# Hybrid streaming encoder step on one core: raw out-projection weights for two blocks, earlier operand loads, and five smaller moves

## The chip, the cores and the metric

The kernel runs on one core of a Trainium2 chip. The metric is the device time of one launch in microseconds, the median of the runs of a kernel. The kernel before has a median of 2514.28 us over three runs (2513.0 to 2514.96).

## The reference, cut to what matters

One layer for 2048 prompt frames and 8 streams of 16 new frames, 2176 tokens in all, in float32, with 1024 channels:

```
z = rmsnorm(x) @ w_in                       # 1280 columns: q 512, k 128, v 128, u 512
a = attention(q, k, v)                      # 8 heads of 64, own chunk of 64 frames + 128 before, sinks
b = pooled means of u (2/4/8/16 frames) - u, a linear map per group, a scale
x = x + concat(rmsnorm(a), rmsnorm(b)) @ w_out
x = x + square(relu(rmsnorm(x) @ w_up)) @ w_down        # 4096 hidden
x = x + sigmoid(rmsnorm(x) @ w_gate) * (p @ w_ple)
y = rmsnorm(x)
```

## The kernel before, in words

**Number format.** Each float32 product is made of three products of rounded halves: a matrix is split into a high part, rounded by ScalarE (a copy into the narrower type), and a low part, the rest, by a subtraction on VectorE or GpSimd. `split` does that for tokens and weights. `mm3` issues the three products of each 128x128 piece of weights. A unit is 128x512 numbers of weights (256 KB raw); its halves together are 512 KB.

**Phase A** (the first 750 us) works on six token blocks (256 and five of 384 tokens). Its steps stand in the string SEQ_A, a letter and a block each: P loads and squares x, I projects (10 output tiles), M takes buffers for the mixer output, A is attention (three tiles of 128 tokens for most blocks, 16 in all), K is pooling, B and R are norms of the mixer outputs, O is the out-projection (8 output tiles d, each of a pool half ps_ob and an attention half ps_oa) that adds x and writes the sum x1 to DRAM (x1d), F is the norm of x1, written to rsd. C0 to C3 (`comb_first`) build columns of the operands of the first up projection: they read x1d and rsd, scale, form sums and differences, split these seven ways and write them to DRAM (cd0). Each C takes the four row buffers xr for its rows and, from C0 to C3, two of the six raw weight buffers wr for the norms.

**Weights in phase A.** `load_w` splits raw weights for blocks 0 and 1. At block 1 it also writes both halves to DRAM (ws...), and blocks 2 to 5 read the halves back without splitting. Raw weights go through six wr buffers into five pairs of wh and wl; halves read back go straight into wh and wl.

**Phase B** works on three pairs of token halves (s = 0, 1, 2; 352 or 368 tokens a half). `up` makes seven products of sums of weights with the seven operands B11, T2, B21, T1, T3, B22, T4 instead of eight, `down` accumulates, `tail` applies the gate (ps_gt) with the embedding product (ps_ple), `finish` the final norm. The loads of the operands of s = 0 (14 tiles of 736 KB) start inside `out_proj(5)`: into buffers of phase B that come free when attention's buffers are released, and two of them into the twelve token buffers q4 of the pool `quads`, which also hold xn and mx.

**PSUM.** ps_ple and ps_gt take three buffers in turn (two mm, one pv) through `ps_dn`; the up products take two sc and two tr in turn.

**Order.** The framework puts each engine's instructions in order at compile time from a timeline of its own (schedule_with_timeline_sim=True), with the order of the program as priority, so the order in a trace is near that of the code, not equal to it. `issue_after` keeps an engine's instructions behind a given one of the same engine. Each engine runs its instructions in that order, and SyncE (SP) issues nearly all DMAs in that order.

Of the kernel before, what the change touches and what calls it, by code (L numbers as in the profile page):

```python
# [7 lines left out]
F32 = mybir.dt.float32  # L8
# [8 lines left out]
P = 128  # L17
# [6 lines left out]
NTOK = SEQ + NSAMP  # L24
BLOCKS = [256, 384, 384, 384, 384, 384]
STARTS = [sum(BLOCKS[:i]) for i in range(len(BLOCKS))]
SEQ_A = "I0 P1 M0 A0 K0 B0 S0 I1 P2 M1 K1 I2 B1 R0 A1 O0 P3 F0 R1 M2 K2 I3 B2 A2 O1 R2 M3 P4 F1 K3 O2 B3 A3 F2 P5 R3 I4 C0 M4 O3 A4 C1 F3 K4 I5 B4 C2 R4 M5 K5 C3 B5 A5 O4"
NXR = 4
TAGS = ("ms ms ms ms ms").split()
LOENG = [lambda nc: nc.vector]  # L30
# [44 lines left out]
def hymba_step(ctx: ExitStack, tc: tile.TileContext, ins, outs):  # L75
# [33 lines left out]
    def ps_tile(tag, nm):  # L109
        return pst.tile([P, 512], F32, tag=tag, name=nm, bufs=PS_BUFS[tag])  # L110

    cnt = [0]
    last_load = [None]

    dn_ring = [0]

    def ps_dn(nm):
        dn_ring[0] += 1
        return ps_tile(("mm", "mm", "pv")[dn_ring[0] % 3], nm)
# [23 lines left out]
    saved = {}  # L143

    def load_w(src, ktiles, key, b):
        if key in saved:
            units = []
            for dh, dl in saved[key]:
                hi = wp.tile([P, 4, P], F32R, tag="wh", name="whi", bufs=NWH)
                lo = wp.tile([P, 4, P], F32R, tag="wl", name="wlo", bufs=NWL)  # L150
                nc.sync.dma_start(out=hi.bitcast(F32), in_=dh)
                nc.sync.dma_start(out=lo.bitcast(F32), in_=dl)
                units.append((hi, lo))
            return WU(units)
        units = [load_u(src[:, k : k + 4, :]) for k in range(0, ktiles, 4)]
        if b == 1:
            saved[key] = []
            for i, (hi, lo) in enumerate(units):
                dh, dl = (dram.tile([P, 4, P], F32, name=f"ws{key}{i}{c}") for c in "hl")
                nc.sync.dma_start(out=dh, in_=hi.bitcast(F32))  # L160
                nc.sync.dma_start(out=dl, in_=lo.bitcast(F32))
                saved[key].append((dh, dl))
        return WU(units)

    def mm3(ps, whl, xs, first=True, last=True):
        n = len(xs)
        for i, (wk, (xh, xl)) in enumerate(xs):
            nc.tensor.matmul(ps, lhsT=whl.hi(wk), rhs=xh, start=first and i == 0, stop=False)  # L168
            nc.tensor.matmul(ps, lhsT=whl.lo(wk), rhs=xh, start=False, stop=False)  # L169
            nc.tensor.matmul(ps, lhsT=whl.hi(wk), rhs=xl, start=False, stop=last and i == n - 1)  # L170

    def ks(xt, N, kk):
        return [(k, (at8(xt[0], k)[:, :N], at8(xt[1], k)[:, :N])) for k in kk]
# [183 lines left out]
    def comb_first(k):  # L357
        wr = lambda dt: lambda nm, n: wp.tile([P, 512], dt, tag="wr", name=nm, bufs=NWR)[:, :n]
        comb(0, k, wr(F32R), wr(F32))

    def out_fin(b):
        rs = state[b]["sq1"].rstd(D, ps_tile("ms", "ps_ms"))
        nc.sync.dma_start(out=rsd[b], in_=rs)

    with tc.tile_pool(name="pa", bufs=2) as pa:
# [122 lines left out]
        def attn_tile(b, i):  # L488
            st_b = state[b]
            gt = TILE0[b] + i  # L490
            q0 = i * P
            qh, ql = st_b["q"]
            kh, kl = st_b["k"]
            first = gt == 0
            J = (1,) if first else (0, 1)
            c0 = 128 if first else 0
            nk = 256 - c0
            st = pa.tile([P, 4, 8], F32, tag="st", name="st")
            rmax, negm, den, esk = (st[:, j, :] for j in range(4))
            pt = []  # L500
            for kv in range(2):
                r = slice(kv * 64, kv * 64 + 64)
                pm = pa.tile([P, NQT, 256], F32, tag="pm", name="pm")
                pt.append(pm)
                for pr in range(2):
                    ps = ps_tile("sc", "ps_sc").rearrange("p (j k) -> p j k", j=2)
                    for j in range(2):
                        t = pr * 2 + j
                        o = ps[:, j, :nk]
                        kk = slice(q0 + c0, q0 + 256)  # L510
                        qq = slice(q0, q0 + 128)
                        nc.tensor.matmul(o, lhsT=qh[r, t, qq], rhs=kh[r, kk], start=True, stop=False)
                        nc.tensor.matmul(o, lhsT=ql[r, t, qq], rhs=kh[r, kk], start=False, stop=False)
                        nc.tensor.matmul(o, lhsT=qh[r, t, qq], rhs=kl[r, kk], start=False, stop=True)
                    for j in range(2):
                        t = pr * 2 + j
                        h = kv * 4 + t
                        nc.vector.tensor_tensor_reduce(
                            out=pm[:, t, :nk], in0=ps[:, j, :nk], in1=mask[:, c0:256], scale=1.0, scalar=NEG,
                            op0=ALU.add, op1=ALU.max, accum_out=rmax[:, h : h + 1],  # L520
                        )
                h4 = slice(kv * 4, kv * 4 + 4)
                nc.vector.scalar_tensor_tensor(
                    out=negm[:, h4], in0=rmax[:, h4], scalar=-0.125, in1=nsink[:, h4], op0=ALU.mult, op1=ALU.min
                )
                nc.vector.tensor_tensor(
                    out=esk[:, h4], in0=negm[:, h4], in1=nsink[:, h4], op=ALU.subtract
                )
                nc.scalar.activation(out=esk[:, h4], in_=esk[:, h4], func=AF.Exp)
                for t in range(4):  # L530
                    h = kv * 4 + t
                    nc.scalar.activation(
                        out=pm[:, t, :nk], in_=pm[:, t, :nk], func=AF.Exp, scale=0.125, bias=negm[:, h : h + 1],
                        accum_out=den[:, h : h + 1],
                    )
                nc.vector.tensor_tensor(out=den[:, h4], in0=den[:, h4], in1=esk[:, h4], op=ALU.add)
                nc.vector.reciprocal(out=den[:, h4], in_=den[:, h4])
                for t in range(4):
                    h = kv * 4 + t
                    nc.scalar.activation(  # L540
                        out=pm[:, t, :nk], in_=pm[:, t, :nk], func=AF.Copy, scale=den[:, h : h + 1]
                    )
            po = ps_tile("pv", "ps_pv")
            nmm = 2 * len(J) * 3
            n = 0
            for kv in range(2):
                for j in J:
                    tp = ps_tile("tr", "ps_tr").rearrange("p (t q) -> p t q", t=NQT)
                    for t in range(4):
                        nc.tensor.transpose(tp[:, t, :], pt[kv][:, t, j * 128 - c0 : j * 128 - c0 + 128], ident)  # L550
                    ph = pa.tile([P, NQT, P], F32R, tag="ph", name="ph")
                    pl = pa.tile([P, NQT, P], F32R, tag="pl", name="pl")
                    split(tp, ph, pl, nc.vector)
                    vi = (gt - 1 + j) % NVP
                    vh = vph[vi][:, kv * 64 : kv * 64 + 128]
                    vl = vpl[vi][:, kv * 64 : kv * 64 + 128]
                    for aa, bb in ((vh, ph), (vl, ph), (vh, pl)):
                        nc.tensor.matmul(po, lhsT=aa, rhs=bb, start=n == 0, stop=n == nmm - 1)
                        n += 1
            put_a(b, po.rearrange("p (t q) -> p t q", t=NQT), q0)  # L560
# [166 lines left out]
        def pool(b):  # L727
# [9 lines left out]

        acts = {
            "P": prologue, "I": in_proj, "M": mixers, "A": attn, "K": pool, "S": lambda b: attn_sample(b, NPR[b]),
            "R": out_ra, "B": out_rb, "O": out_proj, "F": out_fin, "C": comb_first,  # L740
        }
        prologue0()
        consts()
# [3 lines left out]
    with tc.tile_pool(name="pb", bufs=2) as pb:  # L747
# [18 lines left out]

        ops, acc, hq, x2, sqs, rs2 = {}, {}, {}, {}, {}, {}
        up_ring = [0]
        free[Q1] -= 4

        def comb_load(s, names):
            n = HN[2 * s]
            for o in names:
                ops.setdefault(s, {})[o] = (take(o + "h"), take(o + "l"))
                for t, d in zip(ops[s][o], comb_dram[s][o]):
                    nc.sync.dma_start(out=t[:, :, :n].bitcast(F32), in_=d)
# [135 lines left out]
        def tail(s, h, fill=()):  # L914
# [6 lines left out]
            for d in range(KT):  # L921
                if d % 2 == 0:
                    wpl = WU([load_u(w_ple[d // 2], eng=nc.gpsimd)])
                whl = WU([load_u(w_gate[d][:, 4 * i : 4 * i + 4, :], eng=nc.gpsimd) for i in range(2)])
                pe = ps_dn("ps_ple")[:, :n]
                mm3(pe, wpl, [(2 * (d % 2) + k, pt[k]) for k in range(2)])
                ps = ps_dn("ps_gt")[:, :n]
                mm3(ps, whl, xs)
# [38 lines left out]
        def loads(s, names):  # L967
            return [lambda o=o: comb_load(s, [o]) for o in names]

        out_proj(5, loads(0, OPS[:4]))  # L970
        comb_load(0, OPS[4:])
        free[Q1] += 4
        acc_load(0)
        for s in range(3):
# [7 lines left out]
            if s:  # L982
                finish(2 * s - 1)
                acc_load(s)
            else:
                out_fin(4)
                out_fin(5)
            up(s, 2)
            for c in range(NPAIR // 2 - 1):
                down(s, c)  # L990
# [140 lines left out]
```

## Time and profile before

| what | value |
|---|---|
| median of three runs | 2514.28 us |
| the profiled execution, its own time | 2511.46 us |
| its span, first to last instruction | 2509.7 us |
| mean granted TensorE clock | 0.975 |
| matrix products (PE instructions) | 13748 |
| DMA bytes | 370.63 MB |

A page of the profile gives busy times by engine and what ended an engine's idle time. PE is TensorE, DVE VectorE, ACT ScalarE, POOL GpSimd, SPq the DMA queue of SyncE. A wait is put down to the instruction or DMA that came last. The clock is a share of 2.4 GHz.

### The profile page before, as it was taken

The page shows a single profiled execution, that of the slowest core. Times are in us where ns is not written, and L with a number is a line of the kernel's source. Part 1 is how long each engine was busy: PE and PEld are TensorE (multiplying, and loading weights), DVE is VectorE, ACT ScalarE, POOL GpSimd, SP SyncE. Part 2 cuts the span into 40 slices and gives each one's busy share as a digit, 9 for nine tenths or more (in the row PEclk, how much of TensorE's full clock was granted, in tenths as well). Part 3 has the DMA queues.
Part 4 walks back from the last instruction along what each step waited for, and adds up shares of the span by engine and source line. Part 5 has one row for each costly group of instructions (what it writes and reads, how often), then busy time and mean ns, then how long its engine had stood idle before and what let it go on. Part 6 is the DMA issues. An engine that isn't in the chain of part 4 may idle for free.

```text
span 2509.7 us, 38994 instructions
## 1 busy us (share of the span) xinstructions
PE 2354.3 (94%) x13748; PEld 2266.9 (90%) x13748; DVE 1651.0 (66%) x2960; ACT 1025.7 (41%) x2151; POOL 1109.3 (44%) x938
## 2 busy tenths in 40 slices
PE   7789999999769999999999999999999999999986
PEld 7779888887669999999988999999988999999985
DVE  6656676655628777756767677776567766666555
ACT  6437665445413333322644233332354333333353
POOL 5614356342634444433565344443375433333363
PEclk9889999999889999999999999999999999999998
DMA  7945477776892333422644333432445422222232
GB/s 190 305 139 164 159 248 237 236 243 229 282 333 93 122 122 122 134 68 68 224 135 154 94 122 124 127 127 75 133 161 168 134 76 69 76 77 80 71 101 85
DMA packets 242164, 370.63 MB, mean 148 GB/s; under 512 B 43953, under 2 KB 119473, under 8 KB 241969
## 3 DMA queue, kind: packets, MB, share of 16 engines
q1 hardware_dynamic: 241424, 367.42, 45.7%
q8 instruction: 109, 1.79, 0.3%
q14 instruction: 87, 0.70, 0.1%
q10 hardware_dynamic: 544, 0.72, 0.1%
HBM read 298.49 MB, written 69.55 MB: 147 GB/s over the span
## 4 chain that ended last, share of the span: by engine, by line
PE 63%; DVE 14%; DMA 9%; issue 5%; POOL 4%; ACT 4%; SPq 1%; DVEq 0%; POOLq 0%; ACTq 0%
PE ps_dn L168 8%; PE ps_dn L169 8%; PE ps_dn L170 8%; PE ps_up L168 7%; PE ps_up L170 7%; PE ps_up L169 7%; POOL wlo L180 3%; PE ps_in L168 2%; PE ps_in L169 2%; PE ps_in L170 2%; DMA x<-in_xT 2%; DVE wlo L180 2%; DVE x2l L245 1%; DVE acc L856 1%; DMA xc<-x1d 1%
## 5 line engine op out<-in xcount | busy, mean ns | idle before, releaser
L168 PE MATMUL ps_dn<-hh,whi 128*128 128x368 f32 (+1 forms) x1536 | 505.8, 329 | 11.9 <-DVE acc L856 11.3
L169 PE MATMUL ps_dn<-hh,wlo 128*128 128x368 f32 (+1 forms) x1536 | 503.3, 328 | 0.0
L170 PE MATMUL ps_dn<-hl,whi 128*128 128x368 f32 (+1 forms) x1536 | 501.1, 327 | 0.0
L180 POOL TENSOR_TENSOR wlo<-wraw,whi 128x512 fp32r<-128x512 f32 x251 | 343.8, 1373 | 304.0 <-ACT whi L179 245.8
L856 DVE TENSOR_TENSOR acc<-ps_dn,acc 128x368 f32<-128x368 f32 (+1 forms) x384 | 201.8, 531 | 273.2 <-PE ps_dn L170 273.1
L179 ACT CAST whi<-wraw 128x512 fp32r<-128x512 f32 x384 | 236.6, 619 | 330.9 <-PE ps_dn L170 91.0
L168 PEld LDWEIGHTS ps_dn<-hh,whi 128*128 128x128 f32 x1536 | 288.4, 188 | 20.9 <-DVE acc L856 19.5
L180 POOL TENSOR_TENSOR wlo<-A,whi 128x512 fp32r<-128x512 f32 x96 | 127.4, 1327 | 373.2 <-ACT whi L179 268.2
L169 PEld LDWEIGHTS ps_dn<-hh,wlo 128*128 128x128 f32 x1536 | 288.5, 188 | 0.3
L170 PEld LDWEIGHTS ps_dn<-hl,whi 128*128 128x128 f32 x1536 | 288.5, 188 | 0.3
L179 ACT CAST whi<-A 128x512 fp32r<-128x512 f32 x192 | 119.1, 621 | 273.2 <-PE ps_dn L170 185.4
L168 PE MATMUL ps_in<-xnh,whi 128*128 128x384 f32 (+1 forms) x480 | 164.3, 342 | 19.4 <-ACT whi L179 7.7
L198 POOL TENSOR_TENSOR sqa<-sqa,sqt 128x384 f32<-128x384 f32 (+3 forms) x119 | 129.2, 1087 | 92.1 <-ACT sqt L197 84.0
L169 PE MATMUL ps_in<-xnh,wlo 128*128 128x384 f32 (+1 forms) x480 | 163.5, 341 | 1.5 <-DMA wlo<-wsi40l 0.9
L179 ACT CAST whi<-S 128x512 fp32r<-128x512 f32 x144 | 89.2, 620 | 182.8 <-PE ps_dn L170 132.8
L170 PE MATMUL ps_in<-xnl,whi 128*128 128x384 f32 (+1 forms) x480 | 161.0, 337 | 0.2 <-DVE xnl L245 0.2
L168 PE MATMUL ps_gt<-x2h,whi 128*128 128x368 f32 (+1 forms) x384 | 130.8, 341 | 16.3 <-DVE sg L930 8.6
L180 DVE TENSOR_TENSOR wlo<-wraw,whi 128x512 fp32r<-128x512 f32 x133 | 112.9, 849 | 27.3 <-ACT whi L179 22.6
L169 PE MATMUL ps_gt<-x2h,wlo 128*128 128x368 f32 (+1 forms) x384 | 127.7, 332 | 0.0
L170 PE MATMUL ps_gt<-x2l,whi 128*128 128x368 f32 (+1 forms) x384 | 127.3, 332 | 0.0
L792 POOL TENSOR_TENSOR S<-A,S 128x512 f32<-128x512 f32 x48 | 63.2, 1317 | 141.0 <-DVE wlo L180 141.0
L180 DVE TENSOR_TENSOR wlo<-S,whi 128x512 fp32r<-128x512 f32 x144 | 104.9, 728 | 23.7 <-ACT whi L179 19.9
(253 smaller groups left out, 6356.3 us busy)
## 6 DMA issues: line engine op xcount, KB each, us to landing
A<-in_w_up SPq DMA_DIRECT2D x192, 256.0 KB, 2.7
wraw<-in_w_down SPq DMA_DIRECT2D x192, 256.0 KB, 2.6
wraw<-in_w_gate SPq DMA_DIRECT2D x96, 256.0 KB, 2.7
wraw<-in_w_in SPq DMA_DIRECT2D x40, 256.0 KB, 4.6
wraw<-in_w_out SPq DMA_DIRECT2D x32, 256.0 KB, 3.3
x<-in_xT SPq DMA_DIRECT2D x40, 192.0 KB, 3.9
xr<-in_xT SPq DMA_DIRECT2D x40, 192.0 KB, 4.1
x1d<-xr SPq DMA_DIRECT2D x40, 192.0 KB, 3.9
```

Source lines behind the costliest of these rows:

```text
L168: nc.tensor.matmul(ps, lhsT=whl.hi(wk), rhs=xh, start=first and i == 0, stop=False)
L169: nc.tensor.matmul(ps, lhsT=whl.lo(wk), rhs=xh, start=False, stop=False)
L170: nc.tensor.matmul(ps, lhsT=whl.hi(wk), rhs=xl, start=False, stop=last and i == n - 1)
L179: nc.scalar.copy(out=hi, in_=src)
L180: lo_eng.tensor_tensor(out=lo, in0=src, in1=hi.bitcast(F32), op=ALU.subtract)
L198: eng.tensor_tensor(out=o, in0=o, in1=t, op=ALU.add)
L245: eng.scalar_tensor_tensor(out=lo, in0=src, scalar=c, in1=hi.bitcast(F32), op0=ALU.mult, op1=ALU.subtract)
L792: nc.gpsimd.tensor_tensor(out=raw[o], in0=raw[a], in1=raw[b], op=op)
L856: nc.vector.tensor_tensor(out=a, in0=ps, in1=a, op=ALU.add)
```

## The change

Seven edits. (1) For w_out, blocks 4 and 5 split raw weights again; blocks 2 and 3 still read the saved halves. (2) The saved halves of w_in are written at block 2 instead of block 1, so block 2 splits raw weights too. (3) C0 to C3 stand earlier in SEQ_A. (4) A new step L0 in front of O4 loads the operands B11 and T2 of s = 0 into four q4 buffers; `out_proj(5)` then loads the other five operands. (5) The scaling of the attention weights of the second half of the heads goes from ScalarE to VectorE. (6) ps_ple takes sc and tr buffers, so that ps_gt has the other three for itself. (7) The norms F of blocks 4 and 5 are kept, on TensorE, behind the last product of the second `up`.

```diff
-SEQ_A = "... P5 R3 I4 C0 M4 O3 A4 C1 F3 K4 I5 B4 C2 R4 M5 K5 C3 B5 A5 O4"
+SEQ_A = "... P5 R3 C0 I4 C1 M4 O3 C2 A4 C3 F3 K4 I5 B4 R4 M5 K5 B5 A5 L0 O4"
...
-        if key in saved:
+        if key in saved and not (key[0] == "o" and b >= 4):
...
-        if b == 1:
+        if b == (1 if key[0] == "o" else 2):
...
-            nc.tensor.matmul(ps, lhsT=whl.hi(wk), rhs=xl, start=False, stop=last and i == n - 1)
+            last_mm[0] = nc.tensor.matmul(ps, lhsT=whl.hi(wk), rhs=xl, start=False, stop=last and i == n - 1).ins
...
+    pre_ops = {}
+
+    def comb_ahead(s):
+        n = HN[2 * s]
+        for o in OPS[:2]:
+            pre_ops[o] = tuple(
+                quads.tile([P, 4, NMAX], F32R, tag="q4", name=o + c, bufs=NQ1) for c in "hl"
+            )
+            for t, d in zip(pre_ops[o], comb_dram[s][o]):
+                nc.sync.dma_start(out=t[:, :, :n].bitcast(F32), in_=d)
...
-                    nc.scalar.activation(
-                        out=pm[:, t, :nk], in_=pm[:, t, :nk], func=AF.Copy, scale=den[:, h : h + 1]
-                    )
+                    if kv:
+                        nc.vector.tensor_scalar(
+                            out=pm[:, t, :nk], in0=pm[:, t, :nk], scalar1=den[:, h : h + 1], scalar2=None,
+                            op0=ALU.mult,
+                        )
+                    else:
+                        nc.scalar.activation(
+                            out=pm[:, t, :nk], in_=pm[:, t, :nk], func=AF.Copy, scale=den[:, h : h + 1]
+                        )
...
-                pe = ps_dn("ps_ple")[:, :n]
+                pe = ps_tile(("sc", "tr")[d % 2], "ps_ple")[:, :n]
...
-        out_proj(5, loads(0, OPS[:4]))
-        comb_load(0, OPS[4:])
+        out_proj(5, loads(0, OPS[2:6]))
+        comb_load(0, OPS[6:])
...
-                out_fin(4)
-                out_fin(5)
+                with tc.issue_after(last_mm[0]):
+                    out_fin(4)
+                    out_fin(5)
```

## Rows read from the trace of the kernel before

**Rows 1.** The page: the span, and TensorE's busy time (share) and instructions.
```profile
span 2509.7 us, 38994 instructions
...
PE 2354.3 (94%) x13748; PEld 2266.9 (90%) x13748; DVE 1651.0 (66%) x2960; ACT 1025.7 (41%) x2151; POOL 1109.3 (44%) x938
```

**Rows 2.** Busy time by stretch: us; PE, PEld, DVE, ACT, POOL (instructions); clock; DMA share, GB/s.
```profile
597.00:752.00 155.00, 114.85 (x578) 101.94 (x578) 76.52 (x176) 58.86 (x152) 63.90 (x62) 0.88 0.77 274
660.00:752.00 92.00, 65.06 (x334) 61.62 (x333) 32.02 (x51) 14.43 (x27) 37.61 (x35) 0.87 0.95 349
...
425.70:545.40 119.70, 110.25 (x604) 101.48 (x603) 75.71 (x174) 58.31 (x151) 46.85 (x49) 0.96 0.74 239
54.00:118.00 64.00, 51.39 (x281) 48.32 (x280) 45.20 (x77) 31.27 (x70) 41.31 (x37) 0.95 1.02 312
118.00:197.00 79.00, 71.94 (x342) 63.75 (x342) 41.07 (x131) 25.18 (x81) 16.91 (x20) 0.81 0.42 133
...
752.90:815.70 62.80, 62.46 (x371) 61.70 (x370) 52.62 (x80) 22.51 (x43) 27.86 (x21) 1.00 0.29 93
```

**Rows 3.** Chain of work that ended last, 660 to 724 us: start, us, what.
```profile
682.23 8.38 DMA whi<-wso00h
...
690.63 10.64 DMA T1l<-cd0T1l
...
717.26 6.46 DMA whi<-wso21h
```

**Rows 4.** Waits of TensorE, 597 to 752 us: us in total, times, longest.
```profile
PE ps_ms L228 <- POOL sqa L198: 12.7, 1, 12.7
PE ps_ob L168 <- DMA whi<-wso01h: 5.4, 1, 5.4
PE ps_pv L558 <- DVE pl L180: 3.8, 3, 3.1
PE ps_oa L168 <- DVE ot L293: 3.7, 1, 3.7
```

**Rows 5.** DMA issues, 600 to 745 us: engine, op, count, KB each, median us to landing.
```profile
DMA packets 24373, 41.28 MB, mean 285 GB/s; under 512 B 4254, under 2 KB 15006, under 8 KB 24364
...
B11h<-cd0B11h SPq DMA_DIRECT2D x1, 736.0 KB, 6.0
...
B22l<-cd0B22l SPq DMA_DIRECT2D x1, 736.0 KB, 13.2
```

**Rows 6.** VectorE groups, 425.7 to 545.4 us: count, busy, mean ns, idle before, releasers.
```profile
L330 DVE SCALAR_TENSOR_TENSOR xc<-xc,cv_sb,rs 128x368 f32<-128x368 f32 x6 | 5.1, 858 | 11.8 <-DMA xc<-x1d 8.3 <-DMA rs<-rsd 3.1 <-issue 0.4
L180 DVE TENSOR_TENSOR cl<-xc,ch 128x368 fp32r<-128x368 f32 x9 | 4.8, 534 | 1.8 <-ACT ch L179 1.8
```

**Rows 7.** Waits of VectorE, 425.7 to 660 us.
```profile
DVE xc L330 <- DMA xc<-x1d: 16.3, 8, 4.3
```

**Rows 8.** Timeline of SP: the norm of block 2 goes back to the chip.
```profile
472.33 0.32 SPq L320 DMA_DIRECT2D rs<-rsd  x1
```

**Rows 9.** Waits, 54 to 118 us, of ScalarE and of TensorE.
```profile
ACT whi L179 <- DMA wsi21h<-whi: 8.1, 2, 7.5
...
PE ps_pv L558 <- ACT ph L179: 6.4, 2, 6.2
```

**Rows 10.** Groups of the whole run: count, busy, mean ns, idle before.
```profile
L179 ACT CAST whi<-wraw 128x512 fp32r<-128x512 f32 x384 | 236.6, 619 | 330.9 <-PE ps_dn L170 91.0 <-PE ps_up L170 80.5 <-PE ps_gt L170 42.3
L180 POOL TENSOR_TENSOR wlo<-wraw,whi 128x512 fp32r<-128x512 f32 x251 | 343.8, 1373 | 304.0 <-ACT whi L179 245.8 <-DVE v L819 47.3 <-DMA wsi10l<-wlo 4.3
L180 DVE TENSOR_TENSOR wlo<-wraw,whi 128x512 fp32r<-128x512 f32 x133 | 112.9, 849 | 27.3 <-ACT whi L179 22.6 <-DMA wsi01l<-wlo 2.8 <-DMA wso11h<-whi 1.1
L540 ACT ACTIVATE pm<-pm,st 128x256 f32<-128x256 f32 (+1 forms) x128 | 53.8, 492 | 4.8 <-DVE st L537 4.7
```

**Rows 11.** One line each: count, ns min/median/max, first and last start.
```profile
L600 DVE TENSOR_SCALAR sbuf<-sbuf,rm x8: 291/296/298, 125.6 to 175.3; 128x144 f32<-128x144 f32 x8
...
L815 DVE SCALAR_TENSOR_TENSOR x<-x x96: 512/541/1680, 757.5 to 2360.6; 128x368 f32<-128x368 f32 x64, 128x352 f32<-128x352 f32 x32
```

**Rows 12.** Waits of TensorE in the tails, whole run: us in total, times, longest.
```profile
PE ps_ple L168 <- DVE sg L930: 19.4, 12, 3.8
...
PE ps_gt L168 <- DVE sg L930: 8.6, 5, 3.3
```

More of the change, by code (lines that the diff above doesn't have):

```diff
@@ L26 @@
 STARTS = [sum(BLOCKS[:i]) for i in range(len(BLOCKS))]
-SEQ_A = "I0 P1 M0 A0 K0 B0 S0 I1 P2 M1 K1 I2 B1 R0 A1 O0 P3 F0 R1 M2 K2 I3 B2 A2 O1 R2 M3 P4 F1 K3 O2 B3 A3 F2 P5 R3 I4 C0 M4 O3 A4 C1 F3 K4 I5 B4 C2 R4 M5 K5 C3 B5 A5 O4"
+SEQ_A = "I0 P1 M0 A0 K0 B0 S0 I1 P2 M1 K1 I2 B1 R0 A1 O0 P3 F0 R1 M2 K2 I3 B2 A2 O1 R2 M3 P4 F1 K3 O2 B3 A3 F2 P5 R3 C0 I4 C1 M4 O3 C2 A4 C3 F3 K4 I5 B4 R4 M5 K5 B5 A5 L0 O4"
 NXR = 4
@@ L113, in hymba_step @@
     last_load = [None]
+    last_mm = [None]
     dn_ring = [0]
@@ L739, in hymba_step @@
             "P": prologue, "I": in_proj, "M": mixers, "A": attn, "K": pool, "S": lambda b: attn_sample(b, NPR[b]),
-            "R": out_ra, "B": out_rb, "O": out_proj, "F": out_fin, "C": comb_first,
+            "R": out_ra, "B": out_rb, "O": out_proj, "F": out_fin, "C": comb_first, "L": comb_ahead,
         }
@@ L768, in hymba_step @@
         up_ring = [0]
-        free[Q1] -= 4
+        free[Q1] -= 8
+        ops[0] = pre_ops
+        for q in pre_ops.values():
+            for t in q:
+                pool_of[id(t)] = (Q1, t)
         def comb_load(s, names):
```

## The prediction

> **What bounds the kernel now.** I read four views in this order. The page first: TensorE is busy for 94% of the span [rows 1], so time can be won only where it idles or runs at a lower clock. Then the busy times by stretch, to find where that is. From 752.9 to 815.7 us the engine issues 371 products in 62.8 us at clock 1.00 [rows 2], 169 ns each; phase B looks like that nearly throughout. The stretch 597 to 752 us, from block 5's last projections to the end of its out-projection, holds only 578 products in 155 us, at clock 0.88 [rows 2]. At 169 ns scaled from 368 to 384 columns (177 ns) they need 102 us, so at most 53 us can be won there. Third, the chain of waits inside it: from 660 to 724 us the chain is almost only DMA, weights behind operands behind weights [rows 3], and the DMA engines are 95% busy at 349 GB/s [rows 2]. The operands of the up products land 6.0 us after issue at the burst's head and 13.2 us at its tail [rows 5]. Last, the waits by engine: one wait of 12.7 us for a sum on GpSimd, before a norm that the order put in front of block 5's out-projection, then 5.4 us for that projection's first weights [rows 4]; and, in the tails of phase B, VectorE freeing PSUM late [rows 12].
>
> **Edits 1, 4 and 7, around 597 to 752 us.** From 660 us the DMA moves 92 x 0.349 = 32.1 MB. The change takes from it: half of block 5's 16 weight units (16 x 256 KB = 4.2 MB), half of the five units of block 4 loaded after 660 (1.3 MB), and four of the 736 KB operand tiles, loaded earlier into buffers that block 5's input leaves at 597 (3.0 MB). Together 8.5 MB, at 349 GB/s 24 us. Raw units also wait in six buffers wr ahead of the five pairs wh and wl, so more of block 5's weights can be on the chip before the operand burst, which starts when attention's buffers come free; that burst falls from twelve tiles to ten. The norm of 12.7 us goes behind the second up, but alone it would free little: the weights of the next product landed only 5.4 us after it, and the burst had held them [rows 3, 4]. I count it inside the 24 us. Before 660 us, C2 and C3 leave VectorE (edit 3), and TensorE's waits there for low halves and out-projection results are 3.8 + 3.7 us [rows 4], with smaller ones of the same kind behind them; I take 8 back. Sum: 32 us. Bounds: 12 us, block 5's own bytes (4.2 MB) alone; 53 us, every stall gone.
>
> The price of raw weights is 32 units more to split in blocks 4 and 5: ScalarE 32 x 0.619 = 19.8 us, VectorE 16 x 0.849 = 13.6, GpSimd 16 x 1.373 = 22.0 [rows 10]. In this stretch these engines are busy 58.9, 76.5 and 63.9 of 155 us [rows 2]; even in 155 - 32 = 123 us GpSimd stands at 85.9, so I cost it at nothing. If that cover fails (the subtraction comes late for a product), GpSimd's 22.0 us is the price, and GpSimd's adds to x1, queued behind, would be late next. The loads of L0 pass SP's queue ahead of block 4's raw weights; 3.0 MB at 349 GB/s is 8.6 us for which those could be held, while A5 has products to issue. Nothing.
>
> **Edit 3, what the C steps cost where they go.** From 425.7 to 545.4 us (I4 and O3) VectorE is busy 75.7 of 119.7 us and already does 6 of 16 row scalings and 9 of 28 splits of the C steps [rows 2, 6]. All of them there adds 10 x 0.858 + 19 x 0.534 = 18.7 us; the scalings waited 11.8 us for rows and norms, six of them, so ten more wait 19.7; block 4's share of edit 5 adds 12 x 0.296 = 3.6 [rows 6, 11]. VectorE then stands at 117.7 of 119.7 us. It runs in order, so behind a scaling whose row is still in flight stand the evictions of projections, and TensorE waits for those. The added 42 us would have to come from VectorE's free 44, while TensorE idles only 9.4 [rows 2]. Bounds: 0 (all in free time) and 42. I take a loss of 10, a quarter of the added time, nearer to nothing because VectorE's free time is as long as what is added. DMA adds 10 columns' reads and writes here at 74% busy; the same engines moved 349 GB/s elsewhere, so 239 plus some 60 fits.
>
> **Edit 2.** From 54 to 118 us the DMA is full (1.02, 312 GB/s) with block 1's raw weights and 10.5 MB of halves written [rows 2]. ScalarE stood 8.1 us for buffers that such a write still held, and a product of attention waited 6.2 of its 6.4 us for ScalarE in that time [rows 9]. Gain about 8. In block 2's stretch (118 to 197 us, DMA share 0.42) the 10.5 MB written replaces 5.2 MB saved on reading, and 20 units are split: ScalarE 12.4, VectorE 8.5, GpSimd 13.7 us beside 25.2, 41.1 and 16.9 of 79 [rows 2, 10]. The small steps of the sample attention stand behind them in order; I take 4 lost. Net gain 4; bounds 14 gained (the 8.1 and the 6.2 one after another) and 8 lost.
>
> **Edit 5.** ScalarE loses 64 x 0.492 = 31.5 us [rows 10]; VectorE gains 64 such scalings. No such shape is in the trace: the nearest is 144 columns at 296 ns [rows 11], so 19 us. Neither engine ends many waits of TensorE in attention; I take 0, bounds 4 gained, 8 lost. All eight of that row took 291 to 298 ns, while VectorE's instructions with two SBUF inputs reach 1680 ns beside a median of 541 [rows 11]. The Trainium skill (SBUF — State Buffer, "Who interferes with whom") says that VectorE and GpSimd share a port pair as an exclusive lock, and that a tensor_scalar in its two-port mode takes it too. By that rule, which the 1680 ns agrees with and the eight (with GpSimd at 16.9 of 79 us) don't test, these scalings can block and be blocked; the third rival prices it.
>
> **Edit 6.** In the tails TensorE waits 19.4 + 8.6 us for VectorE to read a gate result out of a PSUM buffer [rows 12]: three buffers serve two results per output tile. With seven, TensorE can be some three tiles (of 5 us each) ahead, longer than the longest wait, 3.8 us. The up products, which share sc and tr, may wait for a ps_ple instead. Gain 20 of 28, bounds 0 and 28.
>
> **Sum.** -32 + 10 - 4 + 0 - 20 = -46 us. The profiled execution took 2511.46 us (span 2509.7 and 1.8 around it), so 2465.5; the median of the runs is 2.8 above it, so 2468.
>
> **Rivals.**
> 1. The operand burst still goes ahead of block 5's weights. Ten tiles of 0.754 MB at 349 GB/s are 21.6 us. For it: SP issues in order, and the burst stood in front of these weights before [rows 3]. Against: raw buffers in front of it. The first term is then its lower bound, 12: 2514.3 - 26 = 2488.
> 2. Slower: C0 blocks I4. C0 now stands in front of I4 with priority. Its scalings need block 2's norm, which is read back at 472.33 us [rows 8], while I4 starts at 425.7. If VectorE's queue (or SP's, with I4's weights behind the norm's load) has them first, I4 waits 47 us, and twelve rows of C1 to C3, at the longest wait of 4.3 us each [rows 7], up to 52 more. It decides from 56 us, where the other gains (-32 - 4 - 20) are eaten; with half of the 52 the loss is 73 instead of 10: 2531. Against: the order is laid out at compile time, and before, it kept the third norm load away from other work.
> 3. The lock of that page. If each of 64 scalings waits half of a GpSimd instruction of about 1.37 us in half of the cases [rows 10], VectorE gets 64 x 0.34 = 22 us more in stages where it is the fullest engine after TensorE; at two thirds on the path that is 15: 2483. For it: these stages have GpSimd busy for 46.85 of 119.7 us [rows 2]; against: ScalarE is relieved by more.
> 4. The change doesn't do what it says: C3's last writes come late, so the two wr buffers of its norms and the operands for L0 aren't free in time; the first term is then 12, and the C work crosses O3 and A4 at its upper 42 us. -12 + 42 - 4 - 20 = +6, with edit 6 as it is: 2520, or no change where less of it is on the path.
>
> **How the numbers follow.** Forecast 2468 with 0.57 (own range 2445 to 2490: up to 16 more of the first term and 8 more of the tails one way, some 20 of the C cost the other); the burst 0.18, C0 blocking 0.09, the lock 0.07, late C 0.09. The range 2440 to 2503 leaves out nearly all of the slower case and most of the late C case (0.14 together), and 0.06 at the ends of the forecast's and the burst's own spreads: 2 in 10. About 0.2% (5 us) is what a measurement of this kernel can tell from no change. Slower by more: 0.10 (0.08 of rival 2, 0.02 of rival 4); within: 0.06 (0.05 of rival 4, 0.01 of rival 2); faster: 0.84, the rest.
>
> **What would show it.** Edits 1 and 4: the out-projection of block 5 ends near 720 us instead of 752, with the DMA below 90% busy before that and no wait for weights over 3 us. Edit 7: no wait of ps_ms for GpSimd over 5 us. Edit 2: no ScalarE wait on a weight write in I1. Edit 3: VectorE above 85% busy from I4 to O3, and waits of TensorE for z or ot there. Edit 6: waits for gate results under 10 us in all. I am wrong if that end comes no earlier than 735 us, or if the tails keep their 28.

## The result, and the profile after

The changed kernel takes 2486.05 us (median of four runs, 2480.86 to 2490.34) against 2513.64 us: a ratio of 0.9891, with an interval of 0.987 to 0.9911, or 27.6 us (1.1%) less. The forecast was 2468 (46 less): the direction was right, and the gain came out at three fifths of what I had forecast. The parts behind it are another matter; most of them were off.

The page first: TensorE's busy time and its number of products have not changed against [rows 1], the span has shrunk by 25.2 us, and VectorE carries 59 us more.

```profile
span 2484.5 us, 39054 instructions
...
PE 2357.5 (95%) x13748; PEld 2269.6 (91%) x13748; DVE 1709.9 (69%) x3050; ACT 1026.6 (41%) x2139; POOL 1156.4 (47%) x964
```

Busy time by stretch (us; PE, PEld, VectorE, ScalarE, GpSimd with their instructions; granted clock; DMA share and GB/s). The first five lines run through attention and the out-projections, the last three are the tails of phase B, in which the gates are made, two tails in succession to a line:

```profile
54.00:118.00 64.00, 56.52 (x307) 53.71 (x306) 55.37 (x85) 31.38 (x68) 45.47 (x40) 0.95 0.57 152
118.00:197.00 79.00, 66.94 (x310) 56.57 (x309) 44.27 (x132) 32.91 (x92) 27.60 (x28) 0.81 0.58 193
197.00:312.00 115.00, 107.13 (x641) 93.98 (x642) 87.53 (x257) 75.76 (x217) 41.34 (x47) 0.93 0.47 142
444.00:565.50 121.50, 112.38 (x608) 101.01 (x607) 86.67 (x197) 56.81 (x147) 52.74 (x53) 0.96 0.81 263
636.00:756.00 120.00, 104.62 (x535) 93.94 (x534) 78.41 (x148) 55.59 (x125) 74.80 (x67) 0.93 0.66 229
1246.50:1337.70 91.20, 91.20 (x543) 90.82 (x543) 64.00 (x84) 50.71 (x91) 70.08 (x50) 1.00 0.53 174
1826.10:1917.70 91.60, 90.99 (x544) 90.08 (x543) 65.25 (x84) 50.65 (x91) 69.13 (x50) 1.00 0.53 167
2384.10:2484.00 99.90, 80.77 (x487) 78.35 (x485) 62.99 (x99) 51.05 (x93) 60.37 (x44) 0.92 0.37 114
```

For the third and the last three of these lines the kernel before has, in the same columns and, in the tails, over nearly the same work (its first pair of tails holds 18 products fewer, 525 against 543):

```profile
197.00:312.00 115.00, 111.77 (x698) 99.76 (x697) 77.43 (x236) 83.40 (x232) 47.93 (x56) 0.99 0.51 163
1240.00:1348.00 108.00, 94.70 (x525) 90.72 (x524) 75.10 (x101) 50.16 (x90) 65.38 (x49) 0.95 0.53 170
1831.80:1937.50 105.70, 95.17 (x546) 91.42 (x545) 76.25 (x104) 51.94 (x91) 67.93 (x50) 0.98 0.52 172
2394.70:2509.00 114.30, 86.08 (x488) 79.04 (x486) 66.39 (x99) 52.41 (x93) 57.29 (x44) 0.93 0.31 100
```

Three things are to be seen. The tails are full now: 91.2 us at clock 1.00 where 108.0 at 0.95 stood; the three pairs together take 282.7 us instead of 328.0. The stretch at the turn to phase B is shorter and less crowded: 636 to 756 us, 120 us with the DMA at 66% (69% from 660 us on), where [rows 2] had 155 us at 77% (95% from 660 us on). And attention is slower: from 197 to 312 us, where almost the same work stands in both, 641 products instead of 698, at clock 0.93 instead of 0.99.

One tile view each gives three milestones (count, ns min/median/max, first and last start): the last product of block 5's input projection, the last of its out-projection, the first down product.

```profile
L171 PE MATMUL ps_in<-xnl,whi x480: 279/334/775, 6.7 to 636.4; 128*128 128x384 f32 x133, 128*128 128x256 f32 x27
...
L171 PE MATMUL ps_oa<-mxl,whi x192: 278/334/522, 199.9 to 755.5; 128*128 128x384 f32 x160, 128*128 128x256 f32 x32
...
L169 PE MATMUL ps_dn<-hh,whi x1536: 318/327/443, 791.1 to 2383.6; 128*128 128x368 f32 x128, 128*128 128x352 f32 x64
```

The same three starts in the kernel before, 596.8, 751.8 and 792.5 us:

```profile
L170 PE MATMUL ps_in<-xnl,whi x480: 278/334/629, 7.2 to 596.8; 128*128 128x384 f32 x133, 128*128 128x256 f32 x27
...
L170 PE MATMUL ps_oa<-mxl,whi x192: 278/334/525, 200.2 to 751.8; 128*128 128x384 f32 x160, 128*128 128x256 f32 x32
...
L168 PE MATMUL ps_dn<-hh,whi x1536: 317/328/443, 792.5 to 2394.2; 128*128 128x368 f32 x128, 128*128 128x352 f32 x64
```

So block 5's input ends 39.6 us later than before, its out-projection 3.7 us later, and phase B's down products begin 1.4 us earlier. The 41 us that the turn has gained (from the first milestone to the third, 195.7 us before, 154.7 after) had been lost ahead of it.

The waits of TensorE from 632 to 760 us (us in total, times, longest) answer to [rows 4]:

```profile
PE ps_ob L169 <- DVE ot L291: 3.5, 3, 3.0
PE ps_ob L169 <- ACT sqt L198: 2.8, 1, 2.8
...
PE ps_ms L229 <- POOL sqa L439: 0.8, 1, 0.8
```

The wait of 12.7 us for a sum on GpSimd is gone, and no wait for a transfer of weights is left. Over the whole run two waits have come up:

```profile
PE ps_in L169 <- DVE z L695: 18.1, 8, 5.9
PE ps_up L169 <- ACT x L844: 11.1, 2, 5.5
```

The first stood at 7.3 us before. The second is new: behind the first two pairs of tails an up product waits 5.5 us for ScalarE to copy an earlier one out of its PSUM buffer (L844). No wait of ps_ple or ps_gt for a gate result, the pair of [rows 12], is among the long ones any more. In the chain of work that ended last (start, us, what) the turn still shows transfers, but of raw weights, an operand and x1, where [rows 3] had saved halves and operands in turn:

```profile
704.92 6.20 DMA wraw<-in_w_out
711.13 11.00 DMA T3h<-cd0T3h
722.19 10.68 DMA x1d<-xr
```

And the row that answers to the estimate from [rows 11], the scalings of attention on VectorE, by tile and as a group of the whole run (busy us, mean ns):

```profile
L553 DVE TENSOR_SCALAR pm<-pm,st x64: 273/349/1394, 62.7 to 664.1; 128x256 f32<-128x256 f32 x60, 128x128 f32<-128x128 f32 x4
...
L553 DVE TENSOR_SCALAR pm<-pm,st 128x256 f32<-128x256 f32 (+1 forms) x64 | 31.7, 550 | 0.2
```

### The profile page after: what moved, and what is told of

It is laid out like the page before. It is cut to its first block, busy times and chain, and to the rows that moved or that the text cites. A ratio compares the mean times of both kernels' runs of the same rounds, so it can differ in the third digit from the quotient of the medians.

```text
span 2484.5 us, 39054 instructions
## 1 busy us (share of the span) xinstructions
PE 2357.5 (95%) x13748; PEld 2269.6 (91%) x13748; DVE 1709.9 (69%) x3050; ACT 1026.6 (41%) x2139; POOL 1156.4 (47%) x964
## 4 chain that ended last, share of the span: by engine, by line
PE 51%; DVE 12%; DMA 3%; issue 3%; ACT 2%; POOL 2%; SPq 0%; POOLq 0%; DVEq 0%; ACTq 0%
PE ps_dn L169 8%; PE ps_dn L170 8%; PE ps_dn L171 8%; PE ps_up L169 7%; PE ps_up L171 7%; PE ps_up L170 7%; DVE wlo L181 2%; PE ps_gt L170 2%; PE ps_gt L169 2%; PE ps_gt L171 2%; DVE acc L878 1%; DVE cl L181 1%; DVE x2l L246 1%; DMA xc<-x1d 1%; DVE hl L181 1%
## 5 line engine op out<-in xcount | busy, mean ns | idle before, releaser
L181 POOL TENSOR_TENSOR wlo<-wraw,whi 128x512 fp32r<-128x512 f32 x277 | 379.2, 1375 | 296.3 <-ACT whi L180 227.3
L180 ACT CAST whi<-wraw 128x512 fp32r<-128x512 f32 x436 | 267.5, 617 | 300.0 <-PE ps_dn L171 88.9
L181 DVE TENSOR_TENSOR wlo<-wraw,whi 128x512 fp32r<-128x512 f32 x159 | 138.4, 870 | 24.9 <-ACT whi L180 23.6
L169 PEld LDWEIGHTS ps_in<-xnh,whi 128*128 128x128 f32 x480 | 95.6, 199 | 33.2 <-DVE z L695 14.5
```

What stands on the lines that cost most here:

```text
L180: nc.scalar.copy(out=hi, in_=src)
L181: lo_eng.tensor_tensor(out=lo, in0=src, in1=hi.bitcast(F32), op=ALU.subtract)
```

## The experiments

After this profile I had two theories. The first: edit 6 is worth more than 20 us, and one or more of the edits that put work into attention (5, 2, 3) cost what the turn gives back. Its rival: edit 6 is worth its 20, and what I forecast for the turn did not come. Each of the first four kernels undoes one edit in the changed kernel; the chip's own median of the kernel before stands beside each time, since it moves between 2505.9 and 2513.6 us from one chip to another. Differences are therefore taken between ratios; each ratio carries 0.001 to 0.0025 either way, a difference of two about 0.003 (7 us).

**e1_scale_back**: edit 5 undone.

```
-                    if kv:
-                        nc.vector.tensor_scalar(out=pm[:, t, :nk], ...)
-                    else:
-                        nc.scalar.activation(out=pm[:, t, :nk], ...)
+                    nc.scalar.activation(out=pm[:, t, :nk], ...)
```

> The changed kernel with edit 5 undone: ScalarE scales all heads again. Theory V (the time that the out-projection and tail edits won was partly lost between 200 and 600 us because VectorE got the scalings, 64 x 550 ns = 35 us in the changed kernel's trace, and the C columns): 12 to 18 us faster than the changed kernel, some 2470, and VectorE's busy share from 197 us to the end of block 2's out-projection falls from 71% to about 65%. Theory S (the loss comes from edit 2, whose saves and raw weights in block 2 shift the order of all that follows): within 5 us of the changed kernel's 2486.

Measured: 2469.41 us against 2510.13, ratio 0.9838 [0.9823, 0.9854]. The edit that I had costed at nothing costs 0.0053, some 13 us. Its stretch in the windows view:

```profile
197.00:312.00 115.00, 113.17 (x707) 99.60 (x707) 80.59 (x249) 87.83 (x247) 49.55 (x58) 1.00 0.50 160
```

66 products more than the changed kernel in the same 115 us, at clock 1.00. This does not hang on one execution: in the traces of the six kernels of this study that hold edit 5 (the changed one and those below that undo edits 3, 2, 6, 1 and 7 one at a time) the stretch holds 624 to 649 products, in the eight without it (the kernel before among them) 684 to 707. No trace lies between.

**e2_c_back**: edit 3 undone, the C steps again behind I4, A4, B4 and K5.

```
-... R3 C0 I4 C1 M4 O3 C2 A4 C3 F3 K4 I5 B4 R4 M5 K5 B5 A5 L0 O4
+... R3 I4 C0 M4 O3 A4 C1 F3 K4 I5 B4 C2 R4 M5 K5 C3 B5 A5 L0 O4
```

> The changed kernel with the C steps at their old places in SEQ_A (L0 stays in front of O4). Theory V: the stretch of I4, O3 and I5 (425 to 600 us in the kernel before) gets 10 to 15 us back, but the stretch of O4 and O5 loses the 8 us that VectorE's relief gave it and L0's operands wait for C3's last writes; in all 5 faster to 5 slower than 2486. Theory S: nothing is won before 600 us and the 8 us are lost: 2494 or more.

Measured: 2487.0 us against 2510.13, 0.9908 [0.9889, 0.9926]: the same as the changed kernel. Block 5's input ends at 611.3 us instead of 636.4, and phase B's first down product starts at 797.4 instead of 791.1. What the C steps cost ahead of the turn they free in it.

**e3_save_back**: edit 2 undone.

```
-        if b == (1 if key[0] == "o" else 2):
+        if b == 1:
```

> The changed kernel with edit 2 undone: w_in's halves are saved at block 1 again and block 2 reads them. Theory V: 0 to 6 us slower than 2486, for the 54 to 118 us stretch loses its gain of about 4.5 and block 2 gets most of it back. Theory S: 15 us faster or more, some 2470, with the changed kernel's lag at 300 us gone.

Measured: 2475.42 us against 2510.13, 0.9858 [0.9845, 0.9871]: edit 2 costs 0.0033, 8 us, where I had forecast a gain of 4. Windows of this kernel, to be laid beside the first two of the changed one:

```profile
54.00:118.00 64.00, 53.33 (x293) 51.31 (x292) 46.71 (x89) 29.53 (x66) 39.69 (x37) 0.95 0.98 316
118.00:197.00 79.00, 72.36 (x366) 64.61 (x365) 39.22 (x135) 27.03 (x84) 16.91 (x20) 0.85 0.41 135
```

The DMA is full again in block 1 (0.98 against 0.57), and TensorE issues 14 products fewer there; but in block 2 it issues 366 against 310. So the edit did what it was for in block 1 and took more in block 2, where the splits come on top of the small steps of the sample attention (GpSimd is busy for 27.6 us against 16.9, ScalarE for 32.9 against 27.0, VectorE for 44.3 against 39.2). The 8 us lie between the two theories.

**e4_ple_back**: edit 6 undone.

```
-                pe = ps_tile(("sc", "tr")[d % 2], "ps_ple")[:, :n]
+                pe = ps_dn("ps_ple")[:, :n]
```

> The changed kernel with edit 6 undone: ps_ple and ps_gt share three PSUM buffers again. If the tails' waits for VectorE's reads are what edit 6 took away (30.3 us of waits before, and the last tail's stretch shorter by 19 us in the changed kernel's trace): 20 to 30 us slower than 2486, 2506 to 2516. If the tails became shorter because of other edits (the order that changed with phase A): within 5 us of 2486.

Measured: 2513.85 us against 2510.13, 1.0014 [1.0002, 1.0027]. Without edit 6 the whole change gains nothing. Its waits are those of [rows 12] again:

```profile
PE ps_ple L169 <- DVE sg L952: 19.2, 12, 3.8
...
PE ps_gt L169 <- DVE sg L952: 8.4, 5, 3.3
```

The next four kernels tested the other side: edit 6 alone, the remaining parts of my first term, and whether the two costs add.

**e5_ple_alone**: the kernel before with edit 6 alone (the line of e4, the other way round).

> The kernel before with edit 6 alone. If the tails' gain doesn't depend on the other edits, about 31 us faster than before (that is what undoing it cost), some 2480 on a before of 2511, and phase A's up products start where they did. If edit 6 works only because the other edits change the tails' order: under 15 us faster.

Measured: 2475.49 us against 2508.24, 0.9879 [0.9861, 0.9897]. One line gives 30 us, as much as the whole change. The waits of its tails:

```profile
PE ps_up L168 <- ACT x L822: 11.1, 2, 5.5
```

and the tails by stretch, with the same columns as above:

```profile
1233.60:1326.00 92.40, 91.90 (x546) 90.77 (x545) 65.03 (x84) 50.92 (x92) 69.90 (x50) 1.00 0.52 172
1815.30:1907.00 91.70, 91.24 (x544) 90.32 (x544) 65.32 (x84) 50.61 (x91) 69.07 (x50) 1.00 0.50 167
2371.80:2470.00 98.20, 80.68 (x488) 78.44 (x486) 61.61 (x99) 51.13 (x93) 60.94 (x44) 0.91 0.36 116
```

They sum to 282.3 us against 328.0, 45.7 less; the new wait takes 11.1 back, and 34.6 are left, near the 30 of the timing. Up to the first tail TensorE has the same instructions in the same order in this kernel and in the one before, and yet its first down product starts at 785.2 us instead of 792.5. So 7 us in a milestone of a single execution say nothing.

**e6_halves_back**: edit 1 undone.

```
-        if key in saved and not (key[0] == "o" and b >= 4):
+        if key in saved:
```

> The changed kernel with edit 1 undone: blocks 4 and 5 read w_out's saved halves again (8.4 MB more to load around the operand burst). Theory D (the stretch of O4 and O5 was DMA-bound, and raw weights with the early operands make its gain of some 29 us): 12 to 24 us slower than 2486, with waits of TensorE for ws halves in O5 again. Rival: the gain there is VectorE's relief from the C columns: within 5 us of 2486.

Measured: 2488.69 us against 2508.24, 0.9923 [0.9909, 0.9937]: 0.0032 more than the changed kernel, 8 us. The waits from 560 to 770 us:

```profile
PE ps_ob L169 <- DMA whi<-wso31h: 13.8, 1, 13.8
PE ps_ob L169 <- DMA whi<-wso21h: 6.4, 1, 6.4
```

Block 5's halves are late again, by 20.2 us in two waits, of which 8 us show in the time: between the two theories again. What hides the rest is not shown.

**e7_norms_free**: edit 7 undone.

```
-                with tc.issue_after(last_mm[0]):
-                    out_fin(4)
-                    out_fin(5)
+                out_fin(4)
+                out_fin(5)
```

> The changed kernel with edit 7 undone: nothing holds the norms of blocks 4 and 5 behind the second up. If, as the prediction had it, the wait for the sum covered a wait for weights behind it, 0 to 5 us slower than 2486. If the 12.7 us were a gain of their own: 10 to 13 slower.

Measured: 2482.74 us against 2508.24, 0.9894 [0.9877, 0.9911]: no difference. But the wait of 12.7 us does not come back in this kernel: its longest wait of ps_ms for GpSimd is 0.8 us, as in the changed one, so the order of the other edits keeps that wait away without edit 7. Edit 7 by itself is worth nothing here; what the wait was worth is not tested.

**e8_scale_save_back**: edits 5 and 2 undone together (the diffs of e1 and e3).

> The changed kernel with edits 5 and 2 undone. Undone alone, edit 5 gave 13 us and edit 2 gave 8. If these are separate costs: 20 us under the changed kernel, some 2465. If both act through the same thing, engines too full of small steps between 120 and 420 us: no more than 3 under edit 5's undoing alone, that is 13 to 16 under.

Measured: 2464.92 us against 2508.24, 0.9831 [0.9811, 0.9851]. The two costs do not add: 13 and 8 us alone, 15 together. So edit 5 costs 7 us (0.0027) in a kernel without edit 2 (e3 against this one), and edit 2 costs about 2 in a kernel without edit 5 (e1 against this one). This is the lowest ratio of the study, 43 us under the kernel before and about 15 under the changed one (by the ratios); e1 and the last three below come within 0.0007 of it (2 us), closer than two ratios can tell apart. In its turn no wait is longer than 5.3 us, and none is for a transfer:

```profile
PE ps_in L169 <- DVE z L689: 5.5, 2, 2.8
PE ps_b L169 <- ACT mxh L180: 5.3, 1, 5.3
```

The last four start from e8, so that the costs in attention are out of the way. Open were: how the turn's gain divides over edits 1, 3 and 4, and whether edit 5 costs VectorE's time or a place in its queue.

**e9_no_raw**: e8 with edit 1 undone as well.

> Edits 5, 2 and 1 undone (the run with 5 and 2 undone is the base, ratio 0.983 to before). In the changed kernel, undoing edit 1 brought 20 us of waits for saved halves back but ended phase A at the same time, for other engines were as late. Theory D (raw halves are worth what the DMA frees once phase A no longer lags): 10 to 20 us slower than the base. Theory C (the stretch of O4 and O5 is won by the C columns having left it): within 5 us of the base.

Measured: 2477.22 us against 2505.9, 0.9872 [0.9848, 0.9896]: the raw halves are worth 0.0041, 10 us. One wait shows where:

```profile
PE ps_ob L169 <- DMA whi<-wso31h: 17.3, 1, 17.3
```

**e10_c_late**: e8 with edit 3 undone as well.

> Edits 5, 2 and 3 undone: the C steps at their old places, L0 in front of O4. Theory C: the stretch of O4 and O5 loses most of its gain of 29 us, and the stretch before 600 us gets some 10 back: 12 to 20 us slower than the base. Theory D: 0 to 5 slower.

Measured: 2464.45 us against 2505.9, 0.9833 [0.981, 0.9856]: nothing, in a kernel in which attention is undisturbed. Its milestones (block 5's input, the first down product) are 590.4 and 769.8 us against 606.8 and 764.2 in e8: the earlier C steps cost 16.4 us ahead of the turn and give back 22.0 in it. The 5.6 left are less than two executions differ by.

**e11_no_ahead**: e8 without edit 4, the operands loaded where they were.

```
-... B5 A5 L0 O4
+... B5 A5 O4
...
-        out_proj(5, loads(0, OPS[2:6]))
-        comb_load(0, OPS[6:])
+        out_proj(5, loads(0, OPS[:4]))
+        comb_load(0, OPS[4:])
```

> Edits 5, 2 and 4 undone: no early loads of B11 and T2, all seven operands inside out_proj(5) as before. If the DMA around the burst sets the end of phase A: 3.0 MB more in it at 349 GB/s, some 9 us slower than the base. If it doesn't: within 3.

Measured: 2464.32 us against 2505.9, 0.9836 [0.9811, 0.986]: edit 4 is worth nothing that these runs can tell, where its share of my 24 us would have been 9.

**e12_scale_both**: e1 with 64 scalings of the mask by one added on VectorE, each group of four behind the reciprocal, as many and of the same shapes as edit 5's. They change no value and nothing waits for them; the scalings that attention uses are ScalarE's.

```
+                if kv:
+                    with tc.issue_after(rec.ins):
+                        for t in range(4):
+                            nc.vector.tensor_scalar(out=mask[:, :nk], in0=mask[:, :nk], scalar1=ones[:, 0:1], ...)
```

> Edit 5 undone (ScalarE scales all heads), and VectorE gets 64 instructions of the same kind and size behind the same reciprocals on data that nobody waits for (the mask times one, in place). Theory V1 (edit 5 costs because VectorE's time in attention is full): some 10 to 15 us slower than with edit 5 undone alone, ratio to before near 0.989, and a lag at the start of block 1's out-projection as in the changed kernel. Theory V2 (it costs because the attention weights themselves now wait in VectorE's queue): within 3 us of 0.984.

Measured: 2465.4 us against 2505.9, 0.9834 [0.981, 0.9857], as e1 without them. The added scalings took as long as those of edit 5 (273/353/1382 ns against 273/349/1394):

```profile
L553 DVE TENSOR_SCALAR mask<-mask,ones x64: 273/353/1382, 61.1 to 646.3; 128x256 f32<-128x256 f32 x60, 128x128 f32<-128x128 f32 x4
```

and VectorE was fuller than in the changed kernel in the stretch that edit 5 slows, 90.15 us against 87.53:

```profile
197.00:312.00 115.00, 110.18 (x684) 97.93 (x682) 90.15 (x257) 81.41 (x229) 47.78 (x55) 0.99 0.50 161
```

Yet TensorE issues 684 products there, not 641. So edit 5's cost is not the time that such instructions take on VectorE, with whatever blocks them.

Where the loss arises can be read from two stretches with nearly the same work, 261 products in the changed kernel (first two lines) and 255 in e1:

```profile
239.30:266.90 27.60, 23.90 (x137) 20.14 (x136) 21.94 (x62) 20.11 (x59) 12.07 (x14) 0.94 0.53 167
266.90:298.70 31.80, 27.63 (x124) 22.60 (x123) 23.55 (x71) 18.72 (x54) 7.20 (x8) 0.79 0.32 93
...
237.80:259.20 21.40, 21.36 (x135) 18.52 (x134) 16.04 (x51) 18.65 (x51) 10.99 (x13) 1.00 0.61 196
259.20:283.40 24.20, 22.41 (x120) 18.25 (x119) 17.55 (x52) 22.20 (x63) 7.75 (x9) 1.00 0.47 149
```

They take 59.4 us and 45.6. TensorE stands idle for 7.9 us instead of 1.8, and the rest of the 13.8 us is mostly slower products, at clock 0.94 and 0.79 instead of 1.00 (all at 2.4 GHz). In the changed kernel 1.2 GHz was granted from 249 to 252, from 273 to 283 and from 286 to 290 us; its longest waits in this stretch, 2.1 and 2.6 us, end at 246 and 273 us.

For edit 5's difference to e12 two causes are left: the attention weights themselves stand in VectorE's queue, between its evictions, splits and row scalings; and the order that is laid out at compile time came out otherwise. The first is not borne out. From the reciprocal to the last of the four scaled weights of the second half it took 2.6 us in the changed kernel and 2.8 in e1 and in e12 (means over the 16 tiles), so the weights do not come later. The longest wait of TensorE from 197 to 312 us, for VectorE to read scores out of PSUM, first in the changed kernel, then in e12, looks like the queue:

```profile
PE ps_sc L524 <- DVE st L530: 5.6, 3, 2.6
```

```profile
PE ps_sc L524 <- DVE st L530: 1.2, 1, 1.2
```

But in e3, which holds edit 5 too, it is 0.9 us. The order did change: the last product of block 3's input projection starts at 335.1 us in the changed kernel, at 317.4 and 317.6 in e1 and e12, and the last transpose of the sixth attention tile at 289.1 instead of 301.3 and 306.8. No run moves the scalings and keeps the order, so what makes the 13 us stays open.

## Why the prediction came out as it did

By the ratios, with e5 and e8 as steps in between, the change falls into three parts (in us of 2513.6):

| part | forecast | measured | from |
|---|---|---|---|
| edit 6 | -20 | -30 | 0.9879 - 1 |
| edits 1, 3, 4 and 7 | -32 + 10 = -22 | -12 | 0.9831 - 0.9879 |
| edits 2 and 5 | -4 + 0 = -4 | +15 | 0.9891 - 0.9831 |
| sum | -46 | -27 | 0.9891 - 1 |

The first difference carries some 5 us either way, the two others some 7 each.

**Edit 6: the mechanism right, the size too small.** I had taken 20 of a bound of 28, the two rows of [rows 12]. The bound was no bound. The waits of TensorE in the first pair of tails of the kernel before:

```profile
PE ps_ple L168 <- DVE sg L930: 6.0, 4, 2.5
PE ps_gt L168 <- DVE sg L930: 4.1, 2, 3.3
PE ps_gt L168 <- ACT whi L179: 1.5, 2, 0.7
PE ps_gt L168 <- DVE sg L932: 1.1, 1, 1.1
PE ps_ple L168 <- ACT whi L179: 0.7, 1, 0.7
```

Two of these five rows I had counted, 10.1 of 13.4 us. The pair became 16.8 us shorter, with 18 products more in it: the idle time is gone (13.3 us before), and a product takes 168 ns (91.20 us for 543) instead of 180 (94.70 for 525), at clock 1.00 instead of 0.95. I had not counted the clock. The three pairs lost 45 us, and 11 came back as the new wait of the up products. The prediction had such a wait of theirs, but for a ps_ple. That the mark "under 10 us in all" came true said nothing of the size.

**Edits 1, 4 and 7: the bytes were the wrong measure.** The marks came true (no wait for weights, the DMA below 90%, no wait of ps_ms over 5 us), but not the main one: I had written that I was wrong if the out-projection of block 5 ended no earlier than 735 us, and it ended at 755.5. A part of that is attention's loss; where it is taken away the end comes at 728.4 (e8). The runs put a price on each part: raw halves 8 to 10 us (e6, e9), near the lower bound of 12 from block 5's own bytes; early operands about 0 (e11), not 3.0 MB at 349 GB/s; edit 7 by itself 0 (e7), where the wait that it was for was gone without it. I had turned all bytes that leave a full DMA into time. Here those counted for which TensorE waits, and these were weights of block 5's third and fourth output tiles (wso21h and wso31h in e6, wso31h in e9); no long wait for an operand of the burst shows in e11, which loads all of them as late as before. Rival 1 had put the first term at that bound, and its 2488 is the forecast nearest to the time; but the burst no longer holds these weights, and it is near only since edits 5 and 6 went off by almost as much, one each way.

**Edit 3: the cost came, and so did the gain; both larger than said.** The turn gained 22 us by it and the blocks ahead lost 16 (e10 against e8); I had 8 and 10. In time it is nothing (e2, e10). VectorE did not reach the 85% that I had named: 86.67 of 121.5 us from 444 to 565.5, 71%; the waits for z did come (14.4 us over the whole run in e8 against 5.6 in e10). Neither rival 2 nor rival 4 happened: no block stood still for C0's norm, C3's last write was issued at 606 us and L0's first load at 645, and the row scalings waited 12.1 us for rows from 426 to 660 us, less than the 16.3 of [rows 7].

**Edit 5: the step that failed.** "Neither engine ends many waits of TensorE in attention; I take 0, bounds 4 gained, 8 lost." The measured 13 us lie outside these bounds; in a kernel without edit 2 the cost is 7, just inside, so that the 13 are in part the two edits together, and each figure carries some 6 us either way. I had looked at who ends waits before the change and at busy times, and neither showed the cost: VectorE, busy for 77.4 of 115 us before, was no fuller than ScalarE with 83.4. The scalings kept VectorE busy for 31.7 us against my 19; by e12 that is not what they cost. In place of the 0 the runs show 14 us lost between 239 and 299 us, in idle time and in clock; whether the place of the weights in VectorE's queue brings them or the order that came with it is open.

The Trainium skill (SBUF — State Buffer, "Who interferes with whom") says that a tensor_scalar in a two-port mode takes the port pair that VectorE and GpSimd share, and that whoever comes second blocks fully. The spread in the trace fits the rule, with 273 ns for the shortest, 349 in the middle and 1394 for the longest, but no run here tests it. And e12 has the same durations and none of the loss, so rival 3, which made 15 us of that lock, had the right size by luck: e12 speaks against its reason.

**Edit 2: the sign was wrong in this kernel.** The mark held (DMA share 0.57 in block 1, no wait of ScalarE for a weight write among its longest), TensorE issued 26 products more there than [rows 2] shows, but 32 fewer in block 2. I had put the loss of block 2's small steps at 4 and the gain at 8. It costs 8 beside edit 5 and about 2 without it (e8 against e1); the first is just above what two ratios can differ by, the second well below. That it doesn't gain beside edit 5 is shown; what it does by itself is not.

Two errors of opposite sign thus made the forecast look better than its parts: edit 6 gave 10 more, the six others were to give 26 and in sum cost 3. That the time fell inside the stated range is in part luck.

## What to carry to other kernels

Before a step moves to another engine, do not read a cost of 0 from busy times and from who ends waits today: here both were alike for the two engines, and the move cost 13 us beside edit 2 and 7 without it. Bytes taken off a full DMA were worth only the waits that they ended: price the transfers that TensorE waits for, not the burst. Where two results per tile share a small ring of PSUM buffers, the longest rows of waits underrate what more buffers give, since smaller waits and a lower clock go with them. Of the edits here, 6 and 1 carry the gain (some 30 and 10 of 43 us); 5 and 2 are best left out, and 3, 4 and 7 gave nothing that these runs can tell.

## What the runs showed of the hardware that I had not expected

- A 128x256 float32 tensor_scalar on VectorE took 273 ns at best, 349 in the middle and 1394 at worst, 550 on average, with GpSimd busy for 35 to 71% of the stretches in which it ran; the same spread in scalings whose results nothing waits for came with the same time as without them (e12 and e1, 0.9834 and 0.9838).
- The granted clock of the first pair of tails was 0.95 while no wait in it was longer than 3.3 us, and 1.00 once they were gone; in the third pair it was 0.93 and 0.92.
- Two executions of the same order of TensorE's instructions (before, e5) were 7.3 us apart at the first down product.
